# Weight tiles that begin 120 bytes into buffers of 4352 bytes, in a decoder step bound by TensorE

## Chip, cores and metric

The kernel runs on one core of a Trainium2 chip. The metric is the device time of one execution in microseconds; the kernel before takes 1687.88 us, the median of 3 runs (1686.46 to 1689.45).

## The reference

One inference step of a hybrid decoder layer: 256 prompt tokens and 8 single-token samples, 264 columns in all, width 4096. The input is normalised, projected by one large matrix, mixed by three groups of heads (attention over a window, a matrix memory, a gated MLP over chunks), projected back, added to the input and normalised again. Cut to what matters here:

```python
hn = rmsnorm(h, norm_gain)                     # 264 tokens x 4096
P  = hn @ w_in                                 # 4096 -> 13324 columns, split into the heads' parts
y  = concat(attention(P), mlstm(P), gmlp(P))   # 264 x 4096
h  = h + y @ w_out                             # 4096 -> 4096
out = rmsnorm(h, final_gain)
```

[...]

## The kernel before

The two projections are cut into groups of 512 output columns: `NG` = 26 groups of `w_in` and `NGO` = 8 of `w_out`. A group sums over `KT` = 32 blocks of 128 rows, two blocks (`KK`) to a step, so there are 34 x 16 = 544 steps. For each step, 128 x 2 x 512 weights come in by one transfer of 512 KB (`load_w`, L219, issued by SP, three buffers `wf`). `split_w` (L228) then makes two tiles of them: ScalarE copies them rounded to `wh`, VectorE writes the rest, `wf` minus `wh`, to `wl`. `wh` and `wl` have three buffers each. The activations are kept in the same way as `xh` and `xl` for the whole run, 32 rows of 264 columns, with a row pitch of `ROW` = 320 elements (L72). TensorE then runs, for each of 4 output blocks and 2 row blocks, three matmuls (L1031 to L1033):

```python
PE.matmul(out, wh[:, kk, s], xh[:, k], start=(k == 0), stop=False)
PE.matmul(out, wh[:, kk, s], xl[:, k], start=False, stop=False)
PE.matmul(out, wl[:, kk, s], xh[:, k], start=False, stop=(k == KT - 1))
```

The second operand of the call is the stationary one (the weights, 128 x 128); a load of its own precedes each matmul. The third is the moving one (264 columns). So a step has 24 main matmuls, and the run 13056.

The order of the work is written out by hand (`tc.manual_schedule()`, L104). The loop at L1000 goes over the steps; the transfer of step n + 4 and the split of step n + 2 are issued ahead of the matmuls of step n. Everything else (attention, the matrix memory, the gated MLP, the evacuations) is cut into generators, which `tick` (L331) lets go on between the matmuls, by a small planner that counts the engines' expected times. All operations go through one helper class (L206 is its call), so that nearly every line of the profile is L206 and the tiles' names tell them apart.

Memory is tight: pools of fixed tiles (`cp`, `wp`, `hp`) lie at the bottom of each partition, and a pool `ph` is opened anew for each phase of the run on top of them. The addresses follow from the order of the tiles and the 1024 bytes of scratch at the bottom (L1208). In the built program of before, `xh` starts at byte 1280 of a partition, `xl` at 42240, the three `wf` at 124160, 128256 and 132352, the three `wh` at 136448, 140544 and 144640, and the three `wl` at 148736, 152832 and 156928. `pad0` and `pad1` (L74) are unused tiles that shift what lies behind them.

`rn` (L1097) and `rs` (L1119) are small tiles of the last stage: the factors of the final normalisation, made by `rsqrt` (L270), with which `put` scales the transposed outputs.

Of the kernel before, what the change touches and what calls it, by code (L numbers as in the profile page):

```python
# [10 lines left out]
F32 = mybir.dt.float32  # L11
F32R = mybir.dt.float32r
# [6 lines left out]
P = 128  # L19
D = 4096  # L20
KT = D // P
TP = 256
TS = 8
T = TP + TS
# [42 lines left out]
KK = 2  # L67
# [2 lines left out]
LAG = 6.0  # L70
NCH = KT // KK
ROW = 320  # L72
XOFF = 0
PAD0, PAD1 = 32, 24  # L74

SM = {}
# [15 lines left out]
def body(tc, xt, wi, wg, wo, sm, kc, vc, c0, wst, w00, bs, cgain, cbias,  # L92
         o_y, o_ys, o_kv, o_cp, o_mp, o_cs, o_ms, o_cvp, o_cvs):
    nc = tc.nc
    from contextlib import ExitStack
    with ExitStack() as ctx:
        cp = ctx.enter_context(tc.tile_pool(name="const", bufs=1))
        wp = ctx.enter_context(tc.tile_pool(name="wp", bufs=3))
        hp = ctx.enter_context(tc.tile_pool(name="hp", bufs=1))
# [24 lines left out]
        ph = Phase("ph")  # L124
# [1 line left out]
        keep = Phase("keep")  # L126

        cp.tile([P, PAD0], F32, name="pad0")
        xh = cp.tile([P, KT, ROW], F32R, name="xh")[:, :, XOFF:XOFF + T]
        xl = cp.tile([P, KT, ROW], F32R, name="xl")[:, :, XOFF:XOFF + T]  # L130
        yb = cp.tile([P, KT, T], F32, name="yb")
        sms = cp.tile([P, NSM], F32, name="sms")
        ones = cp.tile([P, P], F32, name="ones")
# [18 lines left out]
        def tt(eng, out, a, b, op):  # L152
            eng.tensor_tensor(out, a, b, op)
# [74 lines left out]
        def split_w(n):  # L228
            if n >= len(steps):
                return  # L230
            t = wf_t.pop(n)
            hi = wp.tile([P, KK, 512], F32R, name="wh")
            lo = wp.tile([P, KK, 512], F32R, name="wl")
            cur[0] = [None, clk["P"]]
            for sl in ((slice(0, 1), slice(1, 2)) if n == 0 else (slice(0, KK),)):
                A.activation(hi[:, sl], t[:, sl], AF.Copy)
                tt(V, lo[:, sl], t[:, sl], hi[:, sl].bitcast(F32), ALU.subtract)
            cur[0] = None
            wh_t[n], wl_t[n] = hi, lo
# [30 lines left out]
        def rsqrt(out, x, scale, v, t):  # L270

            n = out.shape[0]
            V.tensor_scalar(v, x, -0.5 * scale, -0.5 * EPS, ALU.mult, ALU.add)
            A.activation(t, x, AF.Sqrt, scale=scale, bias=epsc[:n, 0:1])
            newton(out, v, t)
# [670 lines left out]
        def final_gain(k):  # L946
            A.activation(yb[:, k], yb[:, k], AF.Copy, scale=sc("fg", k))
# [43 lines left out]
        for i in range(NWARM):  # L991
            PE.matmul(warm[:, :P], ones, ones, start=True, stop=True)
        split_x(0)
        split_w(0)
        load_x(3)
        load_w(3)
        split_x(1)
        split_w(1)
        main_ps = None
        for n, (g, c) in enumerate(steps):  # L1000
# [10 lines left out]
            if g == 0:  # L1011
                split_x(c + 2)
            split_w(n + 2)
            if g == NG:
                for i in (KK * c, KK * c + 1):
# [8 lines left out]
            wh, wl = wh_t.pop(n), wl_t.pop(n)  # L1024
            for j in range(4):
                tick()
                out = main_ps[j][:, :T]
                for kk in range(KK):
                    k = KK * c + kk
# [31 lines left out]
        def state(h):  # L1061
            ps = px.tile([P, 512], F32, name="mx")
            cps[h] = ps
            for b in range(2):
                PE.matmul(ps[:, :DV + 1], st["kws"][:, h, b], st["va"][:, h, b], start=(b == 0), stop=(b == 1))

        def state_out(h):
            A.activation(co[:, h], cps[h][:, :DV + 1], AF.Copy)
            if h in (1, 3, 5):
                nc.scalar.dma_start(o_cp[:, h - 1:h + 1], co[:, h - 1:h + 1])  # L1070

        def turn(q, b):

            ps = pm.tile([P, 512], F32, name="mp")
            for k in range(4):
                tr(ps[:, P * k:P * k + P], yb[:, 4 * q + k, P * b:P * b + P])
            turned[q, b] = ps

        def put(q, b):
            ps, o = turned.pop((q, b)), yo[:, b, 512 * q:512 * q + 512]  # L1080
            if b == 0:
                A.activation(o, ps, AF.Copy, scale=r[:, 0, 0:1])
            else:
                V.tensor_scalar(o, ps, r[:, 0, 1:2], None, ALU.mult)

        def store(q, b, n):
            sl = slice(512 * q, 512 * (q + n))
            DQ.dma_start(o_y[b, :, sl], yo[:, b, sl])
# [4 lines left out]
        for i, a in enumerate(parts):  # L1093
            for b in range(2):
                PE.matmul(ns[:, b:b + 1], a[:, P * b:P * b + P], ones[:, 0:1], start=(i == 0 and b == 0),
                          stop=(i == len(parts) - 1), skip_group_check=True)
        r = hp.tile([P, 3, 2], F32, name="rn")  # L1097
        rsqrt(r[:, 0], ns[:, :2], 1.0 / D, r[:, 1], r[:, 2])
        turn(0, 1)
        turn(1, 0)  # L1100
# [4 lines left out]
        for q in range(NGO):  # L1105
            for b in range(2):
                put(q, b)
                if q < 2 or q == NGO - 1:
                    store(q, b, 1)
                elif q in (3, 5):  # L1110
                    store(q - 1, b, 2)
                elif q == NGO - 2:
                    store(q, b, 1)
            if q >= 2:
                state_out(q - 2)
            if q < 2:
                final_gain(KT - 2 + q)
            if q == 2:
                rs = hp.tile([P, 3, TS], F32, name="rs")  # L1119
                rsqrt(rs[:, 0], nss[:, :TS], 1.0 / D, rs[:, 1], rs[:, 2])  # L1120
                tt(V, yos, yb[:, :, TP:], rs[:, 0].unsqueeze(1).broadcast_to([P, KT, TS]), ALU.mult)
                DQ.dma_start(o_ys, yos)
            if q + 2 < NGO:
                turn(q + 2, 0)
                turn(q + 2, 1)
            if 1 <= q <= MH:
                state(q - 1)
# [100 lines left out]
```

## Time and profile before

| | |
|---|---|
| median of 3 runs | 1687.88 us |
| profiled execution | 1685.23 us |
| its span, first to last instruction | 1683.5 us |
| TensorE busy (matmuls / weight loads) | 99% / 98% |
| VectorE busy | 54% |
| ScalarE busy | 44% |
| GpSimd busy | 4% |
| mean granted TensorE clock | 0.999 |

The busy shares are those of the profiled execution's span. Matmuls follow each other in a pipeline, so a matmul's own duration is longer than the distance to the next, and "99% busy" does not say that the engine is at its peak. The distance from start to start has to be read from counts in windows, from pieces of the chain of waits, or from the timeline.

### The profile page before, as it was taken

To read this page: it belongs to the slowest core of one execution; us is meant where nothing else is said; L and a number is where in the kernel's file an instruction comes from. 1 tells how busy PE (TensorE), PEld (TensorE's weight loads), DVE (VectorE), ACT (ScalarE), POOL (GpSimd) and SP (SyncE) were. 2 spreads that over 40 slices of the span, in tenths; PEclk is the share of its full clock that TensorE was granted. 3 is DMA by queue.
4 is the path that set the end of the run, shared out by engine and by line. 5 is a ranking of instruction groups with operands and counts; after the bars stand their busy time and mean duration, and the time that the engine had idled before them with its cause. 6 is when DMAs were issued, how large, how long until landed. Compare 5 with 4: busy or idle time off the path is not lost.

```text
span 1683.5 us, 32684 instructions
## 1 busy us (share of the span) xinstructions
PE 1670.5 (99%) x13830; PEld 1652.4 (98%) x13830; DVE 901.8 (54%) x1268; ACT 743.5 (44%) x979; POOL 73.2 (4%) x74
## 2 busy tenths in 40 slices
PE   9999999999999999999999999999999999999998
PEld 9999999999999999999999999999999999999997
DVE  6565644655544455555665656444666554444443
ACT  6554433444433433344444444434354443444443
POOL 0000000000000000011001100000100030000000
PEclk9999999999999999999999999999999999999999
DMA  8555668545455655667667666555656666555554
GB/s 300 172 183 175 184 188 277 158 158 165 153 172 180 184 181 185 204 204 241 220 222 238 220 219 223 180 184 181 208 176 217 201 200 195 182 187 178 186 178 159
DMA packets 102372, 328.94 MB, mean 195 GB/s; under 512 B 11155, under 2 KB 23753, under 8 KB 102225
## 3 DMA queue, kind: packets, MB, share of 16 engines
q1 hardware_dynamic: 101648, 326.04, 60.8%
q8 instruction: 108, 1.77, 0.4%
q10 hardware_dynamic: 576, 0.81, 0.1%
q14 instruction: 40, 0.32, 0.0%
HBM read 314.20 MB, written 12.60 MB: 194 GB/s over the span
## 4 chain that ended last, share of the span: by engine, by line
PE 96%; DVE 1%; DMA 1%; ACT 1%; issue 0%; SPq 0%; POOLq 0%; POOL 0%; DVEq 0%; ACTq 0%
PE mp L206 92%; PE mx L206 3%; DVE wl L206 1%; DMA wf<-wo 1%; DMA wf<-wi 0%; PE sn L206 0%; ACT wh L206 0%; PE gps L206 0%; DVE TM L206 0%; PE ns L206 0%; ACT es L206 0%; DVE yb L206 0%; DVE mvs L206 0%; ACT L206 0%; ACT yo L206 0%
## 5 line engine op out<-in xcount | busy, mean ns | idle before, releaser
L206 PE MATMUL mp<-xh,wh 128*128 128x264 f32 x4352 | 1242.7, 286 | 1.4 <-ACT wh L206 0.8
L206 PE MATMUL mp<-xh,wl 128*128 128x264 f32 x4352 | 1232.3, 283 | 3.1 <-DVE wl L206 3.1
L206 PE MATMUL mp<-xl,wh 128*128 128x264 f32 x4352 | 1231.5, 283 | 0.0
L206 DVE TENSOR_TENSOR wl<-wf,wh 128x1024 fp32r<-128x1024 f32 (+1 forms) x545 | 686.9, 1264 | 740.3 <-ACT wh L206 731.3
L206 ACT ACTIVATE wh<-wf 128x1024 fp32r<-128x1024 f32 (+1 forms) x545 | 574.7, 1057 | 807.3 <-PE mp L206 720.4
L206 PEld LDWEIGHTS mp<-xh,wh 128*128 128x128 f32 x4352 | 819.4, 188 | 8.7 <-issue 5.5
L206 PEld LDWEIGHTS mp<-xh,wl 128*128 128x128 f32 x4352 | 819.4, 188 | 4.6 <-DVE wl L206 4.6
L206 PEld LDWEIGHTS mp<-xl,wh 128*128 128x128 f32 x4352 | 819.7, 188 | 0.4
L206 POOL TENSOR_TENSOR acc<-acc,es 128x264 f32<-128x264 f32 x29 | 21.9, 754 | 412.9 <-ACT es L206 410.8
L206 ACT ACT_TABLE_LOAD x22 | 28.2, 1283 | 1.2 <-PEq L1208 0.8
L206 POOL TENSOR_SCALAR_AFFINE_SELECT tmp<-bc 128x128 f32<-128x128 f32 x12 | 5.6, 486 | 490.9 <-DMA bc<-gd 490.9
L206 ACT ACTIVATE es<-yb 128x264 f32<-128x264 f32 x37 | 15.2, 412 | 17.7 <-DVE yb L206 17.7
L206 ACT ACTIVATE bias<-bias,ar 128x128 f32<-128x128 f32 (+1 forms) x24 | 10.7, 448 | 25.0 <-DVE ar L206 24.9
L206 POOL TENSOR_TENSOR cb<-cb,bc 128x2056 f32<-128x2056 f32 x6 | 21.7, 3615 | 0.0
L206 ACT ACTIVATE es<-et 128x264 f32<-128x264 f32 x32 | 12.6, 419 | 17.1 <-DVE yb L206 13.8
L206 DVE SCALAR_TENSOR_TENSOR cb<-vb,wsk,cb 128x257 f32<-128x257 f32 x48 | 20.1, 481 | 0.0
L206 ACT ACTIVATE xh<-yb 128x264 fp32r<-128x264 f32 x32 | 12.1, 412 | 17.7 <-DVE yb L206 17.7
L206 POOL MEMSET pad<- 128x1024 f32 x2 | 1.9, 952 | 410.0 <-PE mx L206 410.0
L206 DVE TENSOR_TENSOR et<-mp,rstd 128x264 f32<-128x264 f32 x52 | 18.8, 425 | 0.0
L206 ACT ACTIVATE yb<-yb,sms 128x264 f32<-128x264 f32 x32 | 16.5, 516 | 0.9
L206 DVE SCALAR_TENSOR_TENSOR xl<-yb,sms,xh 128x264 fp32r<-128x264 f32 x32 | 14.4, 488 | 1.3 <-ACT xh L206 1.2
L206 DVE TENSOR_TENSOR xl<-yb,xh 128x264 fp32r<-128x264 f32 x32 | 12.7, 429 | 3.9 <-ACT xh L206 3.9
(195 smaller groups left out, 474.5 us busy)
## 6 DMA issues: line engine op xcount, KB each, us to landing
wf<-wi SPq DMA_DIRECT2D x415, 512.0 KB, 3.3
wf<-wo SPq DMA_DIRECT2D x128, 512.0 KB, 3.3
cb<-c SPq DMA_DIRECT2D x12, 514.0 KB
o_cs<-cb SPq DMA_DIRECT2D x12, 514.0 KB, 6.4
vb<-vsd SPq DMA_DIRECT2D x12, 512.0 KB, 4.5
yb<-xt SPq DMA_DIRECT2D x34, 132.0 KB, 3.5
yb<-xt SPq DMA_DIRECT2D x15, 264.0 KB, 7.0
Kc<-kc SPq DMA_DIRECT2D x4, 512.0 KB
```

The lines of the kernel that those rows point to most:

```text
L206: return fn(*a, **k)
```

## The change

The weight tiles `wh` and `wl` become flat buffers of 2 x 512 + 64 elements (4352 bytes in place of 4096), of which the weights take the 1024 elements from element 30 on (120 bytes in). `XOFF`, which was 0, goes. The six buffers take 1536 bytes more per partition. The scratch for dynamic transfers is halved to 512 bytes, and `rn` and `rs` move from the pool `hp` to the phase's pool `ph`. All tensors lie 512 bytes lower for the smaller scratch. Nothing else is touched.

```diff
-XOFF = 0
+WOFF = 30
...
-        xh = cp.tile([P, KT, ROW], F32R, name="xh")[:, :, XOFF:XOFF + T]
-        xl = cp.tile([P, KT, ROW], F32R, name="xl")[:, :, XOFF:XOFF + T]
+        xh = cp.tile([P, KT, ROW], F32R, name="xh")[:, :, :T]
+        xl = cp.tile([P, KT, ROW], F32R, name="xl")[:, :, :T]
...
-            hi = wp.tile([P, KK, 512], F32R, name="wh")
-            lo = wp.tile([P, KK, 512], F32R, name="wl")
+            hi, lo = [wp.tile([P, KK * 512 + 64], F32R, name=x)[:, WOFF:WOFF + KK * 512].rearrange(
+                "p (k c) -> p k c", k=KK) for x in ("wh", "wl")]
...
-        r = hp.tile([P, 3, 2], F32, name="rn")
+        r = ph.tile([P, 3, 2], F32, name="rn")
...
-                rs = hp.tile([P, 3, TS], F32, name="rs")
+                rs = ph.tile([P, 3, TS], F32, name="rs")
...
-    nc = _bacc.Bacc("TRN2", target_bir_lowering=False, num_devices=1, dynamic_dma_scratch_size=1024)
+    nc = _bacc.Bacc("TRN2", target_bir_lowering=False, num_devices=1, dynamic_dma_scratch_size=512)
```

## Rows read from the trace of the kernel before

**Rows 1.** The page: span, busy time of PE and loads, clock, chain that ended last.

```profile
span 1683.5 us, 32684 instructions
...
PE 1670.5 (99%) x13830; PEld 1652.4 (98%) x13830; DVE 901.8 (54%) x1268; ACT 743.5 (44%) x979; POOL 73.2 (4%) x74
...
PEclk9999999999999999999999999999999999999999
...
PE 96%; DVE 1%; DMA 1%; ACT 1%; issue 0%; SPq 0%; POOLq 0%; POOL 0%; DVEq 0%; ACTq 0%
PE mp L206 92%; PE mx L206 3%; DVE wl L206 1%; DMA wf<-wo 1%; DMA wf<-wi 0%; PE sn L206 0%; ACT wh L206 0%; PE gps L206 0%; DVE TM L206 0%; PE ns L206 0%; ACT es L206 0%; DVE yb L206 0%; DVE mvs L206 0%; ACT L206 0%; ACT yo L206 0%
```

**Rows 2.** Groups of instructions: count | busy us, mean ns of one | idle before.

```profile
L206 PE MATMUL mp<-xh,wl 128*128 128x264 f32 x4352 | 1232.3, 283 | 3.1 <-DVE wl L206 3.1
L206 PE MATMUL mp<-xl,wh 128*128 128x264 f32 x4352 | 1231.5, 283 | 0.0
L206 PEld LDWEIGHTS mp<-xl,wh 128*128 128x128 f32 x4352 | 819.7, 188 | 0.4
L206 DVE TENSOR_TENSOR wl<-wf,wh 128x1024 fp32r<-128x1024 f32 (+1 forms) x545 | 686.9, 1264 | 740.3 <-ACT wh L206 731.3 <-PE mx L206 7.0 <-DMA wf<-wo 0.5
L206 ACT ACTIVATE wh<-wf 128x1024 fp32r<-128x1024 f32 (+1 forms) x545 | 574.7, 1057 | 807.3 <-PE mp L206 720.4 <-DMA wf<-wo 34.0 <-issue 25.5
...
L206 PE MATMUL mp<-sms,yb 128*128 128x128 f32 x64 | 8.6, 275 | 0.5 <-DVE yo L206 0.4
```

**Rows 3.** Waits of PE: us in total, times, longest us.

```profile
PE mp L206 <- DVE wl L206: 3.1, 7, 1.2
...
PE mp L206 <- ACT wh L206: 0.8, 2, 0.4
```

**Rows 4.** Windows of 40 us, main matmuls alone: first and last of 16.

```profile
60.00:100.00 40.00, 40.00 (x336) 40.00 (x335) 0.00 (x0) 0.00 (x0) 1.00 0.55 171
...
1616.00:1656.00 40.00, 40.00 (x332) 40.00 (x331) 0.00 (x0) 0.00 (x0) 1.00 0.48 153
```

**Rows 5.** Chain in order of time, two whole groups: start us, us, what.

```profile
598.79 46.28 PE mp L206 x385
...
644.96 46.68 PE mp L206 x384
```

**Rows 6.** Timeline of PE and loads: start us, us; two places.

```profile
619.84 0.28 PE L206 MATMUL mp<-xh,wh 128*128 128x264 f32 x1
619.96 0.28 PE L206 MATMUL mp<-xl,wh 128*128 128x264 f32 x1
...
619.84 0.19 PEld L206 LDWEIGHTS mp<-xl,wh 128*128 128x128 f32 x1
...
659.92 0.29 PE L206 MATMUL mp<-xh,wl 128*128 128x264 f32 x1
660.05 0.28 PE L206 MATMUL mp<-xh,wh 128*128 128x264 f32 x1
660.16 0.28 PE L206 MATMUL mp<-xl,wh 128*128 128x264 f32 x1
660.28 0.28 PE L206 MATMUL mp<-xh,wl 128*128 128x264 f32 x1
660.40 0.29 PE L206 MATMUL mp<-xh,wh 128*128 128x264 f32 x1
660.53 0.28 PE L206 MATMUL mp<-xl,wh 128*128 128x264 f32 x1
```

**Rows 7.** Timeline of the tail, PE and loads: eight transposes of the output.

```profile
1663.24 1.07 PE L206 MATMUL mp<-sms,yb 128*128 128x128 f32 x8
...
1663.13 0.94 PEld L206 LDWEIGHTS mp<-sms,yb 128*128 128x128 f32 x8
```

**Rows 8.** DMA queues (packets, MB, share) and an issue that isn't by SP.

```profile
q1 hardware_dynamic: 101648, 326.04, 60.8%
...
q10 hardware_dynamic: 576, 0.81, 0.1%
...
o_cp<-co ACTq DMA_DIRECT2D x3, 257.0 KB
```

**Rows 9.** Timeline of VectorE in the tail: first writes of the two small tiles.

```profile
1663.42 0.16 DVE L206 TENSOR_SCALAR rn<-ns 128x2 f32<-128x2 f32 x1 [1.67 <-PE ns L206]
...
1667.23 0.16 DVE L206 TENSOR_SCALAR rs<-mx 128x8 f32<-128x8 f32 x1
```

## The prediction

> **What bounds the kernel now.** I read the page's totals first, then the chain of waits, then the pace of TensorE itself. [...] PE waits for the splits of the weights for 3.1 + 0.8 us in the whole run [rows 3]. So the time is 13056 times the pace of one matmul, and a change of 1 ns in that pace is 13 us.
>
> The pace has a structure that the page doesn't show. I put windows of 40 us into the 16 projection groups that run for at least 40 us with hardly anything else on PE. Eight of them hold 335 or 336 main matmuls and eight hold 332; the first and the last of the 16 stand in [rows 4]. A matmul that lasts 0.28 us is counted when it touches the window, so a pace is (40 + 0.28)/336 = 119.9 ns or (40 + 0.28)/332 = 121.3 ns. Whole pieces of the chain say the same: 46.28/385 = 120.2 ns and 46.68/384 = 121.6 ns in two groups that follow each other [rows 5]. Where the pace is even, the starts lie 0.12 us apart without exception; where it is uneven, five intervals sum to 0.61 us in place of 0.60, with one of 0.11 among them [rows 6]. Instructions, shapes, buffers and clock are the same in both, and a group keeps its pace until something else is put between the matmuls. I take from this that the kind of pace is a relation in time between two streams that PE reads at once: the moving row of 264 columns and the next 128 columns of weights.
>
> [...] And loads of 128 columns can follow each other faster: in the tail, eight transposes with a load each take 1.07 us, the last of them 275 ns, so (1070 - 275)/7 = 114 ns from start to start [rows 2, 7]. The main loop thus loses some 6 ns in each matmul at the even pace and 7.5 ns at the uneven one.
>
> **The change part by part.** Instructions, their number and their order on each queue stay; none is added or removed, and no wait is added. What moves is addresses.
>
> *Weights.* In the program of before every `wh` and `wl` tile starts 256 bytes above a multiple of 1024, and so, up to multiples of 256, does every row of `xh` and `xl`. After it, the buffers are 4352 bytes apart and the data begin 120 bytes in, so that load and moving row start 120 bytes apart modulo 256, for all 13056 loads. In the trace the load of the next weights starts within 0.02 us of a matmul [rows 6, 7]: today both streams begin at the same place of a 256-byte block at nearly the same moment. The trace of before has no load from another offset, so I bound the effect from both sides. Best end: the pace of the transposes, 114 ns; from a mean of (120.2 + 121.6)/2 = 120.9 that is 6.9 ns x 13056 = 90 us less. Worst end: the load needs one more fetch because its start is not on a round address; at no more than 120.2/128 = 0.94 ns a column, and a fetch of one to four columns, 0.94 to 3.8 ns, or 12 to 49 us more. Between these ends the rows know two values, the two paces. The value nearest to the rows is that the offset breaks the relation that makes the uneven pace, and that the even pace holds throughout: half of the matmuls, 6528, gain 121.56 - 120.21 = 1.35 ns, which is 8.8 us. I take 8.8 us.
>
> *The splits that write and read these tiles.* ScalarE takes 1057 ns and VectorE 1264 ns for a step [rows 2], and a step of 24 matmuls lasts 24 x 120.9 = 2.9 us. No row has them at another offset. A gain there is worth at most the 3.9 us for which PE waits [rows 3]. Should the offset cost them 10%, VectorE needs 1.39 us of 2.9: hidden by the matmuls of the two steps that each split runs ahead. Without that cover the 545 splits would add 545 x 0.13 = 71 us, but VectorE is busy for 54% only, so the cover holds. Taken: nothing. The transfers into `wf` keep their size, and `wf` keeps its place relative to `xh`; nothing.
>
> *Scratch of 512 bytes.* It moves every tensor down by 512 bytes, so `xh` goes from 256 to 768 modulo 1024 and stays at 256 modulo 512. The scratch serves dynamic transfers; the packets of data are on q1 and q10, issued by SP and ScalarE, and no issue by POOL stands in the list [rows 8]. Neither gain nor loss there: nothing.
>
> *`rn` and `rs` in the last phase's pool.* The same two small tiles of 24 and 96 bytes, written first at 1663.42 and 1667.23 us [rows 9], long after the phases that had that space. Should a write have to wait for the end of an older tile's readers, these are drained by then, since the phase is closed after the loop; the wait costs at most the 1.67 us for which VectorE idles before the first of them anyway. Nothing.
>
> Sum: the profiled execution took 1685.23 us (span 1683.5), 2.65 us below the median of 1687.88. 1685.23 - 8.8 = 1676.4; on the scale of the median 1679.
>
> **The rivals.**
>
> *The stall itself goes.* If starting both streams at the same place costs the 6 to 7.5 ns that the main loop has over 114 ns, and not only the 1.35 ns between the paces, the whole gap is open: 90 us, down to 1598. For it: a constant 0.12 us at the even pace, which is no random collision. Against: the moving row is 264 columns and the transposes' 128, so 114 ns may be out of reach. A third of the gap, 30 us, gives 1658.
>
> *Nothing happens.* The two paces may come from the phase of the sequencer after an interposed instruction, which no address touches. Then half the groups stay uneven and the time is 1688, within 0.2% (3.4 us, about what a measurement of this kernel can tell from no change). For it: within an undisturbed group all three buffers of `wh` and of `wl` have the same pace. Against: all of them share their place modulo 256, so they don't test it. [...]
>
> *One more fetch per load (slower).* The place is the weight load, 13056 times. 120 bytes is 30 columns of four bytes; if weights come in units of several columns, the 128 columns now begin and end within a unit. The price is worked out above: 12 us for a column, 49 us for four, so 1700 to 1737. [...] Against: the transposes' 114 ns leave the load 6 ns of slack at the even pace, into which 3.8 ns would fit. [...]
>
> *The uneven pace everywhere (slower).* The offset moves the relation and puts all groups on the wrong side: 8.8 us more, 1697.
>
> **How the numbers follow.** Forecast (even pace throughout) 0.42; the stall itself goes 0.12; nothing 0.21; one more fetch 0.14; uneven pace everywhere 0.11. Faster is 0.42 + 0.12 = 0.54, the same 0.21, slower 0.14 + 0.11 = 0.25. The range from 1645 to 1702 holds the forecast, nothing, the uneven pace, the one-column fetch and the smaller half of the stall's gain; it leaves out the deep gains and the dear fetch. The forecast's own range is 1674 to 1684: the count of uneven groups, and the spread of the runs.
>
> **What would show it.** In windows of 40 us in the undisturbed groups the counts tell everything: 335 or 336 in all 16 is the forecast; 332 in all is the uneven pace; 332 and 336 mixed as now is "nothing"; over 338 is the stall going; under 330 is the extra fetch. The splits should stay at 1057 and 1264 ns to within some per cent, PE's waits for them at some 4 us, and the tail from the last main matmul at the same length. I'm wrong in mechanism if the counts stay mixed and the time still moves, and wrong in sign if loads get a longer distance than now.

## The result, and the profile after

The changed kernel takes 1716.55 us (median of 4 runs, 1715.68 to 1718.57), the one before 1688.6 us beside it (median of 4, 1686.46 to 1689.45): 1.0169 times as long, 95% interval 1.0152 to 1.0187. It is slower by 28 us; the forecast was 9 us faster, and the range ended at 1702.

The page of the kernel after, the lines that answer to [rows 1]: the same number of matmuls, the same shares, the same clock, and a longer span.

```profile
span 1714.6 us, 32685 instructions
PE 1701.3 (99%) x13830; PEld 1684.2 (98%) x13830; DVE 901.9 (53%) x1268; ACT 743.4 (43%) x979; POOL 74.2 (4%) x74
PEclk9999999999999999999999999999999999999999
...
PE 97%; DMA 1%; DVE 1%; ACT 1%; issue 0%; SPq 0%; POOLq 0%; POOL 0%; DVEq 0%; ACTq 0%
```

The busy times of VectorE and ScalarE are those of before to 0.1 us, so the splits cost the same at 120 bytes as at 0 (1264 and 1057 ns for a step in both). The groups of the kernel after, as in [rows 2] (count | busy us, mean ns of one | idle before), show it line by line, and the waits of PE (us in total, times, longest), as in [rows 3], come to 4.1 us in place of 3.9:

```profile
L206 PE MATMUL mp<-xl,wh 128*128 128x264 f32 x4352 | 1244.5, 286 | 0.0
...
L206 PEld LDWEIGHTS mp<-xl,wh 128*128 128x128 f32 x4352 | 829.6, 191 | 0.4
L206 PEld LDWEIGHTS mp<-xh,wh 128*128 128x128 f32 x4352 | 819.2, 188 | 8.4 <-issue 5.6 <-ACT wh L206 1.6
L206 DVE TENSOR_TENSOR wl<-wf,wh 128x1024 fp32r<-128x1024 f32 (+1 forms) x545 | 687.0, 1264 | 770.8 <-ACT wh L206 764.6 <-PE mx L206 5.3
...
L206 ACT ACTIVATE wh<-wf 128x1024 fp32r<-128x1024 f32 (+1 forms) x545 | 574.4, 1057 | 837.5 <-PE mp L206 760.9 <-issue 31.4 <-DMA wf<-wo 19.4
...
PE mp L206 <- DVE wl L206: 2.9, 4, 1.6
PE mp L206 <- ACT wh L206: 1.2, 2, 0.6
```

What moved is the pace. Windows of 40 us in undisturbed groups of the kernel after, main matmuls alone, as in [rows 4] (busy us and count of PE, then of the loads, DVE and ACT, clock, DMA share, GB/s):

```profile
62.00:102.00 40.00, 40.00 (x324) 40.00 (x323) 0.00 (x0) 0.00 (x0) 1.00 0.54 171
...
513.00:553.00 40.00, 40.00 (x336) 40.00 (x335) 0.00 (x0) 0.00 (x0) 1.00 0.59 182
...
1646.00:1686.00 40.00, 40.00 (x323) 40.00 (x323) 0.00 (x0) 0.00 (x0) 1.00 0.48 150
```

Of 16 such windows, one holds 336 matmuls as the even stretches of before, one (whose start lies in other work) 328, and 14 hold 323 or 324: (40 + 0.29)/324 = 124.4 ns. The count of 332 is gone. The pieces of the chain (start us, us, what) say the same for a whole group of each kind, 45.81/381 = 120.2 ns and 46.17/371 = 124.4 ns, beside 120.2 and 121.6 ns in [rows 5]:

```profile
511.55 45.81 PE mp L206 x381
...
605.95 46.17 PE mp L206 x371
```

And the timeline of PE in an uneven stretch of the kernel after (start us, us) has a rhythm of three where [rows 6] has one of five: any three intervals sum to 0.37 or 0.38 us in place of 0.36.

```profile
619.85 0.29 PE L206 MATMUL mp<-xh,wl 128*128 128x264 f32 x1
619.97 0.29 PE L206 MATMUL mp<-xh,wh 128*128 128x264 f32 x1
620.10 0.29 PE L206 MATMUL mp<-xl,wh 128*128 128x264 f32 x1
620.22 0.29 PE L206 MATMUL mp<-xh,wl 128*128 128x264 f32 x1
620.34 0.29 PE L206 MATMUL mp<-xh,wh 128*128 128x264 f32 x1
620.47 0.29 PE L206 MATMUL mp<-xl,wh 128*128 128x264 f32 x1
620.60 0.29 PE L206 MATMUL mp<-xh,wl 128*128 128x264 f32 x1
```

The sum closes. Over all main matmuls that follow each other without a break (less than 150 ns from start to start), the mean distance of starts in the trace is 120.70 ns before and 123.14 ns after; 2.44 ns x 13056 = 31.9 us, and the spans of the two profiled executions differ by 1714.6 - 1683.5 = 31.1 us. (The medians differ by 28 us; the profiled execution of before took 1685.23 us, 3.4 us less than its median.) Of those matmuls 49% run at the even pace of 120.0 ns before and 28% after, counted as even where 30 distances around a matmul average under 120.5 ns; the rest run at 121.3 ns before and at 124.4 ns after. So two things happened: the other pace became longer, and more of the run is at it. By an estimate from these figures, the longer pace over the old share of 51% is (124.4 - 121.3) x 0.51 x 13056 = 21 us, and the rest, some 11 us, is the larger share. The tail is as long as it was: from the first write of `rn` to the end 1714.6 - 1694.44 = 20.2 us, before 1683.5 - 1663.42 = 20.1 us [rows 9].

```profile
1694.44 0.16 DVE L206 TENSOR_SCALAR rn<-ns 128x2 f32<-128x2 f32 x1 [1.70 <-PE ns L206]
```

Where the larger share comes from shows at the starts of the groups. The timeline of PE (start us, us) at one start of before, where the new group's first matmul is the one at 645.04:

```profile
644.91 0.28 PE L206 MATMUL mp<-xh,wl 128*128 128x264 f32 x1
645.04 0.36 PE L206 MATMUL mp<-xh,wh 128*128 128x264 f32 x1
645.24 0.29 PE L206 MATMUL mp<-xl,wh 128*128 128x264 f32 x1
645.36 0.28 PE L206 MATMUL mp<-xh,wl 128*128 128x264 f32 x1
```

And one of the kernel after, where it is the one at 653.20:

```profile
653.08 0.29 PE L206 MATMUL mp<-xh,wl 128*128 128x264 f32 x1
653.20 0.29 PE L206 MATMUL mp<-xh,wh 128*128 128x264 f32 x1
653.32 0.29 PE L206 MATMUL mp<-xl,wh 128*128 128x264 f32 x1
653.45 0.29 PE L206 MATMUL mp<-xh,wl 128*128 128x264 f32 x1
```

I took the group starts that have only main matmuls around them and no longer wait, 19 in each of the two traces. Before, all 19 hold one such long distance, 0.17 to 0.20 us, and behind it the group is even 11 times and uneven 8 times. After, the 4 starts that follow an even stretch hold it too, but the 15 that follow an uneven one hold at most 0.14 us, and all 15 groups go on uneven. The pace of 124.4 ns thus carries over from group to group, which that of 121.3 ns doesn't (of the groups behind such a stretch some go on at 120.0 ns, as the one at 691.71 us). This is a reading of the traces; no run isolates what makes the long distance.

So two questions are left: which part of the change made the uneven pace longer, and what that pace depends on. The experiments are edits of the changed kernel unless said otherwise. The table gathers them; "rows" is how far the moving rows `xh` and `xl` start into their pitch, "share" the part of the main matmuls at the even pace, worked out from each trace as above. In all experiments but e12_before2 no tensor moves against the kernel after except the weights within their buffers and the rows within their pitch. The kernel before took 1685.5 to 1687.0 us (medians) beside them; e5 to e11 and e13 to e15 are single executions, and for those the paces, and not some us in the time, carry the argument.

| run | weights in by | rows in by | time, us | even pace | share | other paces, ns |
|---|---|---|---|---|---|---|
| before | 0 | 0 | 1688.6 | 120.0 | 49% | 121.3 |
| after | 120 B | 0 | 1716.55 | 120.0 | 28% | 124.4 |
| e1_off0 | 0 | 0 | 1686.59 | 120.0 | 53% | 121.3 |
| e3_off2 | 8 B | 0 | 1678.33 | 120.0 | all | none |
| e7_off4 | 16 B | 0 | 1698.03 | 120.0 | 35% | 122.2 |
| e5_off16 | 64 B | 0 | 1681.76 | 120.0 | 89% | some ten distances of up to 132 at a group's start |
| e2_off28 | 112 B | 0 | 1713.19 | 120.0 | 17% | 121.3, 124.4 |
| e6_off32 | 128 B | 0 | 1695.43 | 120.0 | 61% | 123.3 |
| e8_rows30 | 0 | 120 B | 1738.65 | none | 0 | 124.4, 125.0 |
| e4_both30 | 120 B | 120 B | 1732.17 | 120.0 | 9% | 125.0 |
| e15_rows2 | 0 | 8 B | 1711.68 | none | 0 | 122.2, 123.3 |
| e13_both2 | 8 B | 8 B | 1717.68 | none | 0 | 123.3 |
| e14_both32 | 128 B | 128 B | 1688.84 | 120.0 | 49% | 121.3 |
| e11_only_wl | `wh` 0, `wl` 120 B | 0 | 1714.41 | none | 0 | 123.1 |
| e12_before2 | 8 to 168 B | 0 | 1691.85 | none | 0 | 120.5, 121.5, 121.6 in turn |

### The profile page after: what moved, and what is told of

It reads as the page before. It is cut to its first block, busy times and chain, and to the rows that moved or that the text cites. A ratio compares the mean times of both kernels' runs of the same rounds, so it can differ in the third digit from the quotient of the medians.

```text
span 1714.6 us, 32685 instructions
## 1 busy us (share of the span) xinstructions
PE 1701.3 (99%) x13830; PEld 1684.2 (98%) x13830; DVE 901.9 (53%) x1268; ACT 743.4 (43%) x979; POOL 74.2 (4%) x74
## 4 chain that ended last, share of the span: by engine, by line
PE 97%; DMA 1%; DVE 1%; ACT 1%; issue 0%; SPq 0%; POOLq 0%; POOL 0%; DVEq 0%; ACTq 0%
PE mp L206 93%; PE mx L206 3%; DMA wf<-wo 1%; DVE wl L206 0%; PE sn L206 0%; DMA wf<-wi 0%; ACT wh L206 0%; PE gps L206 0%; DVE TM L206 0%; PE ns L206 0%; DVE mvs L206 0%; ACT L206 0%; ACT yo L206 0%; DVE yb L206 0%; ACT co L206 0%
## 5 line engine op out<-in xcount | busy, mean ns | idle before, releaser
L206 PE MATMUL mp<-xh,wh 128*128 128x264 f32 x4352 | 1261.3, 290 | 1.8 <-ACT wh L206 1.2
L206 PE MATMUL mp<-xl,wh 128*128 128x264 f32 x4352 | 1244.5, 286 | 0.0
L206 DVE TENSOR_TENSOR wl<-wf,wh 128x1024 fp32r<-128x1024 f32 (+1 forms) x545 | 687.0, 1264 | 770.8 <-ACT wh L206 764.6
L206 ACT ACTIVATE wh<-wf 128x1024 fp32r<-128x1024 f32 (+1 forms) x545 | 574.4, 1057 | 837.5 <-PE mp L206 760.9
L206 PEld LDWEIGHTS mp<-xh,wl 128*128 128x128 f32 x4352 | 830.6, 191 | 4.1 <-DVE wl L206 4.1
L206 PEld LDWEIGHTS mp<-xl,wh 128*128 128x128 f32 x4352 | 829.6, 191 | 0.4
L206 DVE SCALAR_TENSOR_TENSOR cb<-vb,wsk,cb 128x257 f32<-128x257 f32 x48 | 20.1, 481 | 0.0
```

The costliest lines, as they stand in the source:

```text
L206: return fn(*a, **k)
```

## The experiments

**Which part of the change: the offset alone.** e1_off0 takes the offset back and keeps pitch, scratch and the moved tiles.

```diff
-WOFF = 30
+WOFF = 0
```

> The changed kernel with the offset back at 0; the buffers of 4352 bytes, the smaller scratch and the two moved tiles stay. Theory A (the 8 bytes by which the weights miss a multiple of 16 cost a fetch): about 1688 us, counts per 40 us of 332 to 336. Theory B (the distance of 120 bytes between weights and moving rows modulo 128 or 256 costs it): also about 1688 us. Theory C (the new pitch, or the 512 bytes by which everything moved, costs it): 1717 us, with counts of 324 in most stretches.

1686.59 us beside 1685.6 us, ratio 1.001 (0.9998 to 1.0021), with the counts of before (windows of 40 us of this kernel, two groups):

```profile
508.00:548.00 40.00, 40.00 (x332) 40.00 (x331) 0.00 (x0) 0.00 (x0) 1.00 0.58 181
...
600.00:640.00 40.00, 40.00 (x336) 40.00 (x335) 0.57 (x2) 0.00 (x0) 1.00 0.60 185
```

Theory C is out: the pitch of 4352 bytes, the smaller scratch, the 512 bytes by which all moved and the two small tiles together cost nothing that can be measured. As the pitch puts the buffers 256 bytes apart modulo 512 and 1024 and the paces stay at 120.0 and 121.3 ns, with 53% of the main matmuls even in place of 49%, places of the weights 256 bytes apart were alike in these two kernels.

**Whether it is the 8 bytes beyond a multiple of 16: no.** e2_off28 puts the weights at 112 bytes, a multiple of 16; e3_off2 at 8 bytes, which misses it just as 120 does.

```diff
-WOFF = 30
+WOFF = 28        # e2_off28
+WOFF = 2         # e3_off2
```

> Offset of 28 elements, 112 bytes, a multiple of 16. Theory A: about 1688 us, an uneven pace no longer than 121.3 ns. Theory B: about 1717 us, with stretches at 124.4 ns as in the changed kernel. Theory C: 1717 us.

> Offset of 2 elements, 8 bytes: nearly no distance to the moving rows, but the same 8 bytes off a multiple of 16 as 120. Theory A: about 1717 us with stretches at 124.4 ns. Theory B: about 1688 us. Theory C: 1717 us.

e2_off28 took 1713.19 us, ratio 1.0161 (1.0132 to 1.0191), and e3_off2 1678.33 us, ratio 0.9956 (0.9937 to 0.9976). Theory A had both the wrong way round; theory B had the first about right and missed the second by 10 us. Nor can it be a fetch of another size: 8 bytes would miss the start of any unit above 8 bytes, and 120 is a multiple of 8. Two windows of e2_off28, then the first and the last group of e3_off2 that are undisturbed:

```profile
607.00:647.00 40.00, 40.00 (x324) 40.00 (x323) 0.00 (x0) 0.00 (x0) 1.00 0.55 172
1600.00:1640.00 40.00, 40.00 (x324) 40.00 (x323) 0.00 (x0) 0.00 (x0) 1.00 0.60 187
```

```profile
62.00:102.00 40.00, 40.00 (x336) 40.00 (x335) 0.00 (x0) 0.00 (x0) 1.00 0.59 181
...
1606.00:1646.00 40.00, 40.00 (x335) 39.97 (x334) 1.44 (x4) 0.00 (x0) 1.00 0.51 167
```

With 8 bytes the uneven pace is gone from the whole run. This is the kernel that the forecast described, 335 or 336 in each undisturbed window, at a time within 1 us of it, but at another offset; it is the fastest version here with all its work done. With no uneven stretch left the pace is still 120.0 ns, and no run here holds a shorter one over its main matmuls.

**Both moved by 120 bytes.** e4_both30 brings the distance between weights and rows back to 0.

```diff
-xh = cp.tile([P, KT, ROW], F32R, name="xh")[:, :, :T]
+xh = cp.tile([P, KT, ROW], F32R, name="xh")[:, :, 30:30 + T]      # xl likewise
```

> Weights 120 bytes in and the moving rows 120 bytes in as well, so that their distance modulo 256 is 0 again while both miss a multiple of 16 by 8 bytes. Theory A: 1717 us or more, since the moving rows now miss it too. Theory B: about 1688 us. Theory C: 1717 us.

1732.17 us, ratio 1.0274 (1.0244 to 1.0304), with all but 9% at 125.0 ns. A window of this kernel:

```profile
1614.00:1654.00 40.00, 40.00 (x322) 40.00 (x321) 0.00 (x0) 0.00 (x0) 1.00 0.55 173
```

Theory B, that the distance is all, doesn't get the 1688 us it asked for; the place of the rows has a say as well.

**How the pace goes with the offset.** Three more offsets, and the rows moved alone.

```diff
-WOFF = 30
+WOFF = 16        # e5_off16;  e6_off32: 32;  e7_off4: 4
...
+WOFF = 0         # e8_rows30, with the rows at 30 as in e4_both30
```

> Offset of 16 elements, 64 bytes. Theory D (what counts is where the weights lie within a block of the memory, seen from the moving rows, and the pace repeats with that block): with a block of 64 bytes 1687 us with paces of 120.0 and 121.3 ns; with a block of 128 or 256 bytes a time of its own, 1700 to 1717. Theory E (only few bytes of distance matter, since they set how many columns the two reads are apart at the start, and any long distance is bad): 1713 to 1717 us.

> Offset of 32 elements, 128 bytes. Theory D with a block of 64 or 128 bytes: 1687 us and both paces of the kernel before. Theory D with 256 bytes, or theory E: 1713 to 1717 us, stretches at 124.4 ns.

> Offset of 4 elements, 16 bytes. Theory D with a block of 16 bytes (8 bytes were good because they are half of one): 1687 us, as offset 0. Theory E: about 1678 us, as the offset of 8 bytes, since the distance is short too.

> Weights at offset 0, moving rows 120 bytes in. If the place of the moving rows by itself made the 1732 us of the run with both moved (theory R): about 1732 us, pace 125.0 ns. If only the distance between the two counts, whatever its sign (theory D): 1713 to 1717 us.

Times of 1681.76, 1695.43, 1698.03 and 1738.65 us beside 1686.98. No expectation holds for the three offsets: 64 bytes are better than 0, though theory E had long distances bad and theory D had them equal to 0 or worse; 16 bytes are worse than 0 and than 8; 128 bytes are not like 0 and have stretches of their own at 123.3 ns (326 in the second window below, where offset 0 has 332), so no block of 64 or 128 bytes repeats. For the rows alone, theory R comes close: 125.0 ns for most of the run, with or without the weights' move. Two windows of e6_off32, then one each of e7_off4 and e8_rows30:

```profile
607.00:647.00 40.00, 40.00 (x336) 40.00 (x335) 0.00 (x0) 0.00 (x0) 1.00 0.59 182
559.00:599.00 40.00, 40.00 (x326) 40.00 (x326) 0.12 (x1) 0.00 (x0) 1.00 0.58 183
...
515.00:555.00 40.00, 40.00 (x330) 40.00 (x329) 0.00 (x0) 0.00 (x0) 1.00 0.60 182
...
617.00:657.00 40.00, 40.00 (x323) 40.00 (x321) 1.45 (x4) 0.00 (x0) 1.00 0.56 175
```

**Whether it is PE alone.** The weight tiles are also written by ScalarE and VectorE and fed by transfers. e9_quiet30 and e10_quiet0 take all of that away for 541 of the 544 steps, once with the offset of 120 bytes and once with none.

```diff
         def load_w(n):
-            if n >= len(steps):
+            if n >= 3:
                 return
...
         def split_w(n):
-            if n >= len(steps):
+            if n >= 3:
+                wh_t[n], wl_t[n] = kept[n % 3]
                 return
```

> Offset of 120 bytes as in the changed kernel, but the weights of the first three steps are used in every step: no transfer, no copy on ScalarE and no subtraction on VectorE for the other 541 steps, so the outputs are those of other weights. Theory P (the two reads of PE alone make the long pace): stretches at 120.0 and at 124.4 ns as in the changed kernel. Theory W (writes into the weight tiles, or their transfers, get in the way of PE's reads): 120.0 ns, or some other single pace, throughout.

> The same without offset. Theory P: stretches at 120.0 and at 121.3 ns as in the kernel before, 28 us or so less than with the offset if as many stretches are long as there. Theory W: one pace, the same as with the offset.

The paces are those of the full kernels to the count. Two windows of e9_quiet30 and two of e10_quiet0; the DMA shares of 0.00 show how quiet it is:

```profile
607.00:647.00 40.00, 40.00 (x336) 40.00 (x335) 0.00 (x0) 0.00 (x0) 1.00 0.00 1
1100.00:1140.00 40.00, 40.00 (x324) 40.00 (x323) 0.00 (x0) 0.00 (x0) 1.00 0.00 1
```

```profile
250.00:290.00 40.00, 40.00 (x332) 40.00 (x331) 0.00 (x0) 0.00 (x0) 1.00 0.26 91
...
598.00:638.00 40.00, 40.00 (x336) 40.00 (x335) 0.00 (x0) 0.00 (x0) 1.00 0.00 1
```

The first window of e10_quiet0 still has a transfer for other work in its first 10 us (share 0.26). So here are 30 us of the same uneven stretch with all instructions counted (PE, loads, VectorE, ScalarE, GpSimd, clock, DMA share, GB/s): 249 matmuls, where 120.0 ns would give 252, and nothing else at work.

```profile
262.00:292.00 30.00, 30.00 (x249) 30.00 (x248) 0.00 (x0) 0.00 (x0) 0.00 (x0) 1.00 0.00 1
```

Theory W is out: 120.0 and 124.4 ns (e9_quiet30), and 120.0 and 121.3 ns (e10_quiet0), stand at a DMA share of 0.00 with no weight tile being written. The times are 1691.78 and 1674.40 us, 17 us apart and not 28, since more of the run is even (61% and 71%). The share is thus set by something else than the offset alone. Groups that follow each other keep one pace here: in e9_quiet30 the windows of five in a row hold 335 or 336 main matmuls (514 to 738 us), and those of three others 323 or 324 (1051 to 1187 us).

**Whether each load has its price: no.** e11_only_wl moves `wl` only.

```diff
-[:, WOFF:WOFF + KK * 512].rearrange("p (k c) -> p k c", k=KK) for x in ("wh", "wl")]
+[:, o:o + KK * 512].rearrange("p (k c) -> p k c", k=KK) for x, o in (("wh", 0), ("wl", WOFF))]
```

> Only wl lies 120 bytes in, wh at 0. Theory L (each load has its price by its own place): a third of the excess over 120.0 ns that the changed kernel has, a pace of about (2 x 121.3 + 124.4)/3 = 122.4 ns in the uneven stretches, some 1697 us. Theory S (three loads in a row settle into one rhythm, which depends on all of them): a pace that is no such mean, anywhere from 120.0 to 124.4 ns.

1714.41 us, the whole loss with a third of the loads moved. There is one pace, 123.1 ns (327 in the windows), and no even stretch at all. Theory L is out: by it the uneven stretches would be at 122.4 ns beside even ones. The 123.1 ns over all three loads fit theory S, in which a rhythm depends on all of them; no run shows the price of a single load.

```profile
617.00:657.00 40.00, 40.00 (x327) 40.00 (x326) 1.44 (x4) 0.00 (x0) 1.00 0.58 175
1600.00:1640.00 40.00, 40.00 (x327) 40.00 (x326) 0.00 (x0) 0.00 (x0) 1.00 0.62 189
```

**The kernel before with 8 bytes and a small pitch.** e12_before2 was to get the gain without the memory that the change had to find.

```diff
-            hi = wp.tile([P, KK, 512], F32R, name="wh")
-            lo = wp.tile([P, KK, 512], F32R, name="wl")
+            hi, lo = [wp.tile([P, KK * 512 + 8], F32R, name=x)[:, 2:2 + KK * 512].rearrange(
+                "p (k c) -> p k c", k=KK) for x in ("wh", "wl")]
```

> The kernel before with only this edit: weights 8 bytes into buffers of 4128 bytes, scratch and small tiles as before. The six buffers then lie 8, 40, 72, 104, 136 and 168 bytes beyond a multiple of 256. If only the last 32 bytes of the address count: 120.0 ns throughout, 1678 us, as the offset of 8 bytes had it. If the place within 256 bytes counts: stretches at several paces over 121 ns, 1690 to 1710 us.

1691.85 us, ratio 1.0038 (1.0024 to 1.0052): slower than before, with 331 to 333 in the windows and no even stretch. More than the last 32 bytes of the address counts, so a pitch of 4128 bytes, which gives the six buffers six places, loses what 8 bytes alone had won. The pace goes with the buffers from step to step: in the trace the median step of 24 matmuls runs at 120.5 ns with one of the three pairs of `wh` and `wl`, and at 121.5 and 121.6 ns with the two others. A window of this kernel:

```profile
602.00:642.00 40.00, 40.00 (x332) 40.00 (x331) 0.21 (x1) 0.00 (x0) 1.00 0.60 184
```

**Distance or place.** The last three move both by 8 bytes, both by 128 bytes, and the rows alone by 8.

```diff
+WOFF = 2     rows at 2      # e13_both2
+WOFF = 32    rows at 32     # e14_both32
+WOFF = 0     rows at 2      # e15_rows2
```

> Weights and moving rows both 8 bytes in: distance 0. Theory G (the distance alone sets the paces): 120.0 and 121.3 ns, about 1687 us, as in the kernel before. Theory H (the moving rows have a price of their own when they start off a round address, on top of what the weights' place does): paces over 122 ns, 1715 to 1738 us.

> Weights and moving rows both 128 bytes in: distance 0, and both on a multiple of 128. Theory G: 120.0 and 121.3 ns, about 1687 us. Theory H, with round meaning a multiple of 16 to 128 bytes: also 1687 us, where weights alone at 128 bytes had 1695 us with stretches at 123.3 ns.

> Only the moving rows 8 bytes in, weights at 0. Theory G: distance of -8, not tried yet, a pace of its own from 120.0 to 122.2 ns, 1677 to 1700 us. Theory H: over 122 ns, 1715 to 1738 us.

1717.68, 1688.84 and 1711.68 us beside 1686.27. Both by 128 bytes is the kernel before again, 49% even and the rest at 121.3 ns, while 128 bytes for the weights alone was not: so for rows on a multiple of 128, as far as these runs go, the distance decides. Rows 8 bytes in never reach the even pace, with the weights at 0 or at 8 (123.3 ns at distance 0): the rows' own place counts as well, as theory H has it, though its time for the rows alone, 1715 to 1738, came out 3 us lower. Windows of e14_both32, then of e13_both2 (two) and e15_rows2:

```profile
600.00:640.00 40.00, 40.00 (x332) 40.00 (x331) 1.34 (x4) 0.00 (x0) 1.00 0.59 178
647.00:687.00 40.00, 40.00 (x335) 40.00 (x334) 0.99 (x3) 0.00 (x0) 1.00 0.58 184
```

```profile
615.00:655.00 40.00, 40.00 (x326) 40.00 (x325) 0.00 (x0) 0.00 (x0) 1.00 0.59 182
1600.00:1640.00 40.00, 40.00 (x327) 40.00 (x326) 0.00 (x0) 0.00 (x0) 1.00 0.58 181
...
513.00:553.00 40.00, 40.00 (x326) 40.00 (x326) 1.45 (x4) 0.00 (x0) 1.00 0.55 173
```

## Why the prediction was wrong, step by step

*The bound.* Right: the whole difference lies in the pace of the main matmuls, 31.9 us by the starts and 31.1 us by the spans. That the pace is a relation between two streams that PE reads was an inference. The quiet pair shows that PE makes both paces by itself (120.0 ns, and 124.4 or 121.3 ns, at a DMA share of 0.00), and weights and rows moved together by 128 bytes bring back the paces of before, 120.0 and 121.3 ns, where the weights alone at 128 bytes have 120.0 and 123.3 ns. The remark that a group keeps its pace until something else is put between the matmuls holds within a group, but in the kernel before the pace also changes at group starts with no other instruction of PE between, behind one long distance of 0.17 to 0.20 us.

*The size and sign of the weights' term.* This is the step that failed: "The value nearest to the rows is that the offset breaks the relation that makes the uneven pace, and that the even pace holds throughout", 8.8 us less. The trace of before held the two paces of one distance, 0, and I read them as the only two there are. They aren't: the even pace of 120.0 ns recurs in most layouts, and the other belongs to the layout: 121.3 ns at 0 bytes, 122.2 at 16, 123.3 at 128, 124.4 at 112 and 120, none at 8. So in place of 8.8 us less the offset brought 28 us more (31.9 us by the starts): the uneven pace became 124.4 ns, and its share rose from half to 72% of the matmuls. The excess over 120.0 ns grew from 0.70 to 3.14 ns. That the place of the weights matters was right; the direction was guessed, since nothing in one layout's rows says which way another goes. That 8 bytes gave the forecast's time is luck and no merit of it.

*The bounds.* From 114 ns (90 us less) to 49 us more, they held the result, 28 us more. The range cut the upper one to a single column's price, and all prices of the extra fetch, 12 to 49 us, got 0.14 between them; that was too little for a term that rested on no row: a fetch of one to four columns was an assumption, and no run shows one.

*The splits, the scratch, the pitch, the two small tiles, the tail.* Nothing, as predicted: 1057 and 1264 ns, waits of 4.1 us, a tail of 20.2 us from the first write of `rn`, and e1_off0 at ratio 1.001.

*The rivals.* "One more fetch per load" has the measured time among its prices and is still not the cause: 8 bytes beyond a multiple of 16 is the best place found (120.0 ns throughout), and 112 bytes, on a multiple of 16, has the same 124.4 ns as 120. "Nothing happens" fell with the counts: moving the weights alone takes the long pace from 121.3 to 124.4 ns, also where no other engine and no transfer is at work, and how much it does depends on where the rows lie (with the rows 120 bytes in, 125.0 ns holds for most of the run with the weights at 0 as at 120). "The uneven pace everywhere" came nearest in kind: 72% of the matmuls in place of all, at 124.4 ns where I priced 121.6. "The stall itself goes" was seen nowhere: even without a single uneven stretch the pace is 120.0 ns.

*What stays open.* Why 8 bytes is a good distance (120.0 ns) and 16 a bad one (122.2 ns for most of the run), what makes the long distance of 0.17 to 0.20 us at a group's start and picks the pace that a group settles into behind it, and what holds the even pace at 120.0 ns over the 114 ns of the transposes. That the two reads of PE get in each other's way fits all the runs, but none of them shows it directly: they give the paces by place, not the circuit behind them.

## What to carry to other kernels

When matmuls with a fresh load each fill the time, read their distance from counts in equal windows before anything else: in the kernel before, two paces of the same instructions, 120.0 and 121.3 ns, stood at a layout that did matter, but they didn't say which layout is better. Such a knob is to be measured, in steps as small as 8 bytes and with the other operand held still, and its forecast needs a range of the size of the effect (here 60 us between the best and the worst place) with both signs open. Buffers that take turns should all lie at the place that was measured as good, modulo 256 bytes: in e12_before2 the pace went with the buffer from step to step (120.5 ns with one pair, 121.5 and 121.6 with the others), and a bad place for a third of the loads cost as much here as for all (1714.41 us in e11_only_wl, 1716.55 us after).

## What the runs showed of the hardware that was not expected

The start addresses of the two operands within 256 bytes changed the pace of a stream of matmuls of 264 columns with loads of 128: 120.0 to 125.0 ns on the same instructions at the same clock (1.00 in the windows), 1678 to 1739 us. Places of the weights 256 bytes apart were alike (120.0 and 121.3 ns in e1_off0 as before), places 128 bytes apart were not (120.0 and 123.3 ns in e6_off32), unless the rows moved along (120.0 and 121.3 ns in e14_both32). Moving rows 8 bytes in held 122.2 and 123.3 ns (e15_rows2, e13_both2), and rows 120 bytes in 124.4 and 125.0 ns (e8_rows30, e4_both30) but for 9% of the matmuls of e4_both30. The paces are sharp: 120.0 ns, 606.7 ns for five matmuls at offset 0 in the trace of before and 373.3 ns for three at 120 bytes in that of after, the same in every stretch. They survive where PE alone works, at a DMA share of 0.00: 324 main matmuls in 40 us in e9_quiet30, 249 in 30 us in e10_quiet0. A pace can also carry over: in the kernel after, the 15 uneven groups behind an uneven stretch start without the long distance (at most 0.14 us) that the 4 starts behind an even one have, and stay uneven.
